# Macaron decoder layer on one core: an attention pipeline with one more step between its first two stages, projection pieces spread over its end, and the convolution's weights loaded behind it

## The chip, the core and the metric

The kernel runs on one core of a Trainium2 chip. The metric is device time in microseconds (us) from the first to the last work of one execution, as the median of three runs. The profile is of a single execution.

## What is computed

One layer of a decoder: SwiGLU feed-forward, a token mixer with two branches, a second feed-forward, each behind an RMSNorm with adaptive shift and scale. The change is in the mixer's attention branch and in the merge of the two branches:

```python
proj = h @ w_in[l]                                   # h: normalised, (1, 1024, 1024)
b_g, c_g, u, q, k, v, z_conv, z_attn = jnp.split(proj, IN_OFFSETS, axis=-1)
y_conv = (b_g * short_conv(c_g * u, conv_w[l])) @ w_conv_proj[l]
q = apply_rope(q.reshape(bsz, s, 16, 64), cos, sin)
k = apply_rope(k.reshape(bsz, s, 4, 64), cos, sin)
y_attn = sliding_window_attention(q, k, v, sinks[l]) @ w_attn_proj[l]
merged = jax.nn.sigmoid(z_conv) * y_conv + jax.nn.sigmoid(z_attn) * y_attn
x = x + gt2[:, None, :] * (merged @ w_out[l])
```

The attention looks back over a window of 128 positions, in blocks of 128 queries; 4 key-value heads serve 16 query heads, and each head has a sink in its softmax.

## The kernel before

All products are float32. Each operand is split into a high and a low part (`split`, L105 to L107: a cast on ACT, then a subtraction on DVE or POOL), and a product is three matmuls (`mm3`, L134 to L142). A weight block of 128 x 1024 comes by `load_w`: SP loads it into a landing buffer with the tag `wr` (four buffers), then two casts and two subtractions write its parts into two other tiles. The landing buffer is free again when the second subtraction is done.

The attention stage runs over 32 units, (g, n): key-value head g and query block n, with n inner. A unit goes through five stages. A (`stage_a`) multiplies the block by the q, k and v weights of the head, DVE applies the rotary factors to the result in PSUM, and POOL adds the two halves (L995) and copies a piece (L996). B (`stage_b`) transposes that on PE (L1010) and splits it. C (`stage_c`) makes the scores (L1031) and the softmax: four rows of DVE (L1042), four of ACT (L1048), then POOL divides (L1060). D (`stage_d`) transposes the probabilities (L1074) and splits them. E (`stage_e`) multiplies by v (L1097, L1098) and splits the result into tiles (L1108, L1109) that four units fill together.

When four units have filled such a tile, eight projection pieces are put into the list `fill`: one piece (`proj_piece`) is 12 matmuls for one of eight output rows db, with weights from a block that serves four pieces; the result is added to `yat` on DVE (L1128). The loop over steps s issues for each step C of unit s-2, B of unit s-1, A of unit s, two pieces, E of unit s-4 and D of unit s-3. Here C(30) stands for C of unit 30, and so on. `conv_proj` (24 matmuls) multiplies the convolution branch by its weights (`load_wc`: four blocks at a time) and merges both branches on DVE with gates that SP loads (L1155 to L1157); `load_y` brings the convolution branch back from DRAM, eight tiles of 512 KB a half.

PE's order is the order of the code. That of DVE, ACT, POOL and SP is worked out when the kernel is built; each engine then takes its rows in that order. Tiles of a tag go to whichever buffer is free.

Of the kernel before, what the change touches and what calls it, by code (L numbers as in the profile page):

```python
# [35 lines left out]
def tile_macaron_layer(  # L36
# [19 lines left out]
    nc = tc.nc  # L56
# [22 lines left out]
    def tile_t(dt=F32R, shape=(P, 2, HALF)):  # L79
        return act.tile(list(shape), dt, tag="T", name=nm("t"), bufs=28)  # L80
# [14 lines left out]
    def f32(t):  # L95
        return t.bitcast(F32)
# [34 lines left out]
    def load_w(src, lo_engine=nc.vector, tiles=None):  # L131
        return Weights(load_st(src), src.shape[1], lo_engine, tiles)
# [821 lines left out]
    with tc.tile_pool(name="att", bufs=2) as tmp:  # L954
# [48 lines left out]
        def stage_b(g, n):  # L1003

            u = st[g, n]
            if n == 0:
                kts[g] = tile_c(F32R), tile_c(F32R)
            o = bank()
            for i in range(3):
                nc.tensor.transpose(  # L1010
                    o[:, i * P : (i + 1) * P], u["r"][:, i * P : (i + 1) * P], ident
                )
            qt = sum_tile(HALF, F32R)
            qh, ql = qt[:, 0:256], qt[:, 256:512]
            split(qh, ql, o[:, 0:256])
            kh, kl = (t[:, n * P : (n + 1) * P] for t in kts[g])
            split(kh, kl, o[:, 256:384])
            u["q"] = (qh, ql)
# [92 lines left out]

        wapt = {}

        def proj_piece(g, h, db):

            if db % 4 == 0:
                wapt[0] = load_w(wap[g, db // 4], nc.gpsimd if db == 0 else nc.vector,
                                 [tile_t(), tile_t()])
            o = bank()
            ah, al = at[g, h]  # L1120
            for pr in range(2):
                c0 = pr * 512 + (db % 4) * P
                mm3([o], wapt[0](c0), [(ah[:, pr, :], al[:, pr, :])],
                    pr == 0, pr == 1)
            if g == 0:
                nc.scalar.copy(yat[db][h], o)
            else:
                nc.vector.tensor_tensor(yat[db][h], yat[db][h], o, op=ALU.add)  # L1128
# [5 lines left out]
        def load_y(h):  # L1134
            for i in range(KT):
                t = tile_t()
                nc.sync.dma_start(f32(t), ycv[i][h])
                yparts[i, h] = pair_of(t)

        def load_wc(dq):  # L1140
            wc[dq] = [load_w(wcp[g, dq]) for g in range(4)]
# [20 lines left out]

        units = [(g, n) for g in range(NKV) for n in range(NB)]
        fill = []
        for s in range(len(units) + 4):
            def at_(k):
                return units[s - k] if 0 <= s - k < len(units) else None
            if at_(2):
                stage_c(*at_(2))
            if at_(1):  # L1170
                stage_b(*at_(1))
            if at_(0):
                g, n = at_(0)
                if n == 0:
                    load_group(g)
                stage_a(g, n)
            if s == len(units):
                load_wc(0)
                load_y(0)
                load_y(1)  # L1180
            for _ in range(2):
                if fill:
                    proj_piece(*fill.pop(0))
            if at_(4):
                stage_e(*at_(4))
                g, n = at_(4)
                if n % 4 == 3:
                    fill += [(g, n // 4, db) for db in range(8)]
            if at_(3):
                stage_d(*at_(3))  # L1190
            if s > len(units):
                conv_proj(s - len(units) - 1, 0)
        for f in fill:
            proj_piece(*f)
        conv_proj(3, 0)
        for db in range(4):
            conv_proj(db, 1)
# [208 lines left out]
```

## Time and profile before

| | |
|---|---|
| median of 3 runs | 2294.13 us (2292.82 to 2300.34) |
| the profiled execution | 2291.84 us, span of its instructions 2289.7 us |
| PE busy | 2206.0 us, 96% of the span |
| DVE, ACT, POOL busy | 1675.7, 1061.9, 395.0 us (73%, 46%, 17%) |
| attention stage, first A to last piece | about 1096 to 1468 us of the span |
| mean granted TensorE clock | 0.988 |

The attention stage is 16% of the span. The shares are means over the whole kernel: where PE waits is read from its list of waits and its timeline.

### The profile page before, as it was taken

The page shows a single profiled execution, that of the slowest core. Times are in us where ns is not written, and L with a number is a line of the kernel's source. Part 1 is how long each engine was busy: PE and PEld are TensorE (multiplying, and loading weights), DVE is VectorE, ACT ScalarE, POOL GpSimd, SP SyncE. Part 2 cuts the span into 40 slices and gives each one's busy share as a digit, 9 for nine tenths or more (in the row PEclk, how much of TensorE's full clock was granted, in tenths as well). Part 3 has the DMA queues.
Part 4 walks back from the last instruction along what each step waited for, and adds up shares of the span by engine and source line. Part 5 has one row for each costly group of instructions (what it writes and reads, how often), then busy time and mean ns, then how long its engine had stood idle before and what let it go on. Part 6 is the DMA issues. An engine that isn't in the chain of part 4 may idle for free.

```text
span 2289.7 us, 30099 instructions
## 1 busy us (share of the span) xinstructions
PE 2206.0 (96%) x10392; PEld 1845.3 (81%) x10392; DVE 1675.7 (73%) x2966; ACT 1061.9 (46%) x2095; POOL 395.0 (17%) x445
## 2 busy tenths in 40 slices
PE   5899999999998999999899997999999999999997
PEld 3688888888887888888889996788888888888786
DVE  8897778767868777777477776554786776676876
ACT  4554444444446443343476555123644444454443
POOL 3000000006452000000344443002100000002644
PEclk9899999999999999999999998999999999999998
DMA  8265456599732543444121115454233553389932
GB/s 322 74 221 172 149 185 212 181 406 299 270 115 106 184 134 107 155 157 155 56 64 57 49 48 212 133 170 155 75 120 120 184 184 120 120 326 343 337 116 74
DMA packets 146744, 381.63 MB, mean 167 GB/s; under 512 B 20384, under 2 KB 22560, under 8 KB 146592
## 3 DMA queue, kind: packets, MB, share of 16 engines
q1 hardware_dynamic: 141984, 371.33, 46.5%
q0 software_dynamic: 4608, 8.39, 2.1%
q8 instruction: 81, 1.33, 0.2%
q14 instruction: 71, 0.58, 0.1%
HBM read 270.61 MB, written 109.05 MB: 166 GB/s over the span
## 4 chain that ended last, share of the span: by engine, by line
PE 86%; DVE 7%; issue 2%; ACT 1%; DMA 1%; POOL 1%; SPq 0%; POOLq 0%; DVEq 0%; ACTq 0%
PE ps L195 60%; PE ps L142 6%; PE ps L140 6%; PE ps L138 6%; PE ps L977 2%; PE ps L975 2%; PE ps L976 2%; DVE w L107 1%; PE ps L1031 1%; PE ps L1074 1%; DVE t L225 1%; DMA wr<-in_w2d_dram 1%; POOL s L319 1%; PE ps L1010 1%; PE ps L1098 1%
## 5 line engine op out<-in xcount | busy, mean ns | idle before, releaser
L195 PE MATMUL ps<-t,w 128*128 128x512 f32 x6468 | 1469.2, 389 | 5.0 <-DVE r L405 3.0
L195 PEld LDWEIGHTS ps<-t,w 128*128 128x128 f32 x6468 | 1213.4, 188 | 260.4 <-DVE r L405 5.8
L106 ACT CAST w<-wr 128x512 fp32r<-128x512 f32 (+1 forms) x420 | 255.3, 613 | 481.2 <-PE ps L195 365.3
L107 DVE TENSOR_TENSOR w<-wr,w 128x512 fp32r<-128x512 f32 (+1 forms) x404 | 304.4, 760 | 137.8 <-ACT w L106 136.2
L515 POOL TENSOR_TENSOR x<-x,g 128x512 f32<-128x512 f32 x96 | 145.2, 1526 | 1061.5 <-DMA t<-hs 941.1
L106 ACT CAST w<-ws 128x512 fp32r<-128x512 f32 x231 | 143.9, 623 | 250.3 <-PE ps L195 200.6
L140 PE MATMUL ps<-t,w 128*128 128x512 f32 (+1 forms) x528 | 204.9, 388 | 6.5 <-DVE t L290 6.5
L107 DVE TENSOR_TENSOR w<-ws,w 128x512 fp32r<-128x512 f32 x231 | 161.4, 703 | 39.4 <-ACT w L106 39.0
L138 PE MATMUL ps<-t,w 128*128 128x512 f32 (+1 forms) x400 | 156.2, 390 | 7.2 <-ACT t L279 7.2
L142 PE MATMUL ps<-t,w 128*128 128x512 f32 (+1 forms) x400 | 154.4, 386 | 1.1 <-DVE w L107 1.1
L140 PEld LDWEIGHTS ps<-t,w 128*128 128x128 f32 x528 | 100.4, 190 | 28.4 <-DVE t L290 9.2
L344 DVE TENSOR_TENSOR x<-x,x 128x512 fp32r<-128x512 f32 x161 | 102.8, 687 | 2.9 <-ACT x L343 2.8
L343 ACT CAST x<-x 128x512 fp32r<-128x512 f32 x161 | 88.8, 624 | 20.4 <-DVE x L431 10.2
L225 DVE CUSTOM_DVE_ANT_0 wr<-wr,crow_act,v 128x1024 f32<-128x1024 f32 x56 | 71.7, 1282 | 36.0 <-DMA wr<-in_wada_dram 35.9
L138 PEld LDWEIGHTS ps<-t,w 128*128 128x128 f32 x400 | 76.4, 191 | 23.9 <-ACT t L279 9.8
L569 DVE SCALAR_TENSOR_TENSOR x<-ps,mods,x 128x512 f32<-128x512 f32 (+1 forms) x104 | 72.9, 706 | 23.6 <-PE ps L195 12.9
L107 POOL TENSOR_TENSOR w<-wr,w 128x512 fp32r<-128x512 f32 (+1 forms) x16 | 21.5, 1358 | 397.3 <-ACT w L106 397.3
L142 PEld LDWEIGHTS ps<-t,w 128*128 128x128 f32 x400 | 76.4, 191 | 16.5 <-DVE w L107 1.8
L319 POOL TENSOR_TENSOR s<-s,q 128x512 f32<-128x512 f32 (+1 forms) x48 | 56.8, 1185 | 188.8 <-ACT q L315 187.3
L975 PE MATMUL ps<-w,t 128*128 128x384 f32 x256 | 88.3, 345 | 0.0
L977 PE MATMUL ps<-w,t 128*128 128x384 f32 x256 | 85.7, 335 | 0.0
L976 PE MATMUL ps<-w,t 128*128 128x384 f32 x256 | 85.6, 335 | 0.0
(150 smaller groups left out, 2815.6 us busy)
## 6 DMA issues: line engine op xcount, KB each, us to landing
t<-hs SPq DMA_DIRECT2D x140, 512.0 KB, 9.9
hs<-x SPq DMA_DIRECT2D x277, 256.0 KB, 4.6
wr<-in_wada_dram SPq DMA_DIRECT2D x56, 512.0 KB, 3.8
wr<-in_w1gu_dram SPq DMA_DIRECT2D x44, 512.0 KB, 4.6
wr<-in_w2gu_dram SPq DMA_DIRECT2D x44, 512.0 KB, 3.6
wr<-in_wbcu_dram SPq DMA_DIRECT2D x24, 512.0 KB, 4.1
wr<-in_w1d_dram SPq DMA_DIRECT2D x22, 512.0 KB, 7.5
wr<-in_w2d_dram SPq DMA_DIRECT2D x22, 512.0 KB, 7.5
```

Source lines behind the costliest of these rows:

```text
L106: nc.scalar.copy(hi, src)
L107: lo_engine.tensor_tensor(lo, src, f32(hi), op=ALU.subtract)
L138: mm(o, wh, xh, start=start, stop=False)
L140: mm(o, wh, xl, start=False, stop=False)
L142: mm(o, wl, xh, start=False, stop=stop)
L195: mm(o, a, b, start=first, stop=last, skip_group_check=True)
L225: nc.vector.tensor_tensor_reduce(out=st, in0=st, in1=crow_act, scale=1.0, scalar=v[:, C_BADA + i : C_BADA + i + 1], op0=ALU.mult, op1=ALU. ...
L344: nc.vector.tensor_tensor(f32r(t), t, f32(hi), op=ALU.subtract)
L515: nc.gpsimd.tensor_tensor(dst, dst, r, op=ALU.add)
L975: mm(o[:, :384], xh, wh, start=k == 0, stop=False)
L976: mm(o[:, :384], xh, wl, start=False, stop=False)
L977: mm(o[:, :384], xl, wh, start=False, stop=k == KT - 1)
```

## The change

Three parts. The loop has one step more between A and B: a step now issues C of unit s-3, B of unit s-2, A of unit s, the pieces, E of unit s-5 and D of unit s-4. The pieces are two a step up to step 28, one a step from step 29 to 32, three a step from 33 to 36. A weight block for pieces is now asked for one block ahead (`next_wap`), right behind the fourth piece of the block before it, and its low part is always made by DVE (before, every second block's was made by POOL). And at the end: `load_y(0)` moves from step 32 to step 29, `load_wc(0)` and `load_y(1)` stand behind the loop, and the first two `conv_proj` stand behind the loop as well, ahead of the last eight pieces, where before the first three were issued in steps 33 to 35.

```diff
--- before.py
+++ after.py
@@ -1111,17 +1111,21 @@
 
         wapt = {}
 
+        def next_wap(g, h, db):
+            wapt["next"] = load_w(wap[g, db // 4], tiles=[tile_t(), tile_t()])
+
         def proj_piece(g, h, db):
 
             if db % 4 == 0:
-                wapt[0] = load_w(wap[g, db // 4], nc.gpsimd if db == 0 else nc.vector,
-                                 [tile_t(), tile_t()])
+                wapt[0] = wapt.pop("next")
             o = bank()
             ah, al = at[g, h]
             for pr in range(2):
                 c0 = pr * 512 + (db % 4) * P
                 mm3([o], wapt[0](c0), [(ah[:, pr, :], al[:, pr, :])],
                     pr == 0, pr == 1)
+            if db % 4 == 3 and fill:
+                next_wap(*fill[0])
             if g == 0:
                 nc.scalar.copy(yat[db][h], o)
             else:
@@ -1162,36 +1166,41 @@
 
         units = [(g, n) for g in range(NKV) for n in range(NB)]
         fill = []
-        for s in range(len(units) + 4):
+        n_units = len(units)
+        for s in range(n_units + 5):
             def at_(k):
-                return units[s - k] if 0 <= s - k < len(units) else None
+                return units[s - k] if 0 <= s - k < n_units else None
+            if at_(3):
+                stage_c(*at_(3))
             if at_(2):
-                stage_c(*at_(2))
-            if at_(1):
-                stage_b(*at_(1))
+                stage_b(*at_(2))
             if at_(0):
                 g, n = at_(0)
                 if n == 0:
                     load_group(g)
                 stage_a(g, n)
-            if s == len(units):
-                load_wc(0)
+            if s == n_units - 3:
                 load_y(0)
-                load_y(1)
-            for _ in range(2):
+
+            for _ in range(2 if s < n_units - 3 else 1 if s <= n_units else 3):
                 if fill:
                     proj_piece(*fill.pop(0))
+            if at_(5):
+                stage_e(*at_(5))
+                g, n = at_(5)
+                if n % 4 == 3:
+                    if not fill:
+                        next_wap(g, n // 4, 0)
+                    fill += [(g, n // 4, db) for db in range(8)]
             if at_(4):
-                stage_e(*at_(4))
-                g, n = at_(4)
-                if n % 4 == 3:
-                    fill += [(g, n // 4, db) for db in range(8)]
-            if at_(3):
-                stage_d(*at_(3))
-            if s > len(units):
-                conv_proj(s - len(units) - 1, 0)
-        for f in fill:
-            proj_piece(*f)
+                stage_d(*at_(4))
+        load_wc(0)
+        load_y(1)
+        conv_proj(0, 0)
+        conv_proj(1, 0)
+        while fill:
+            proj_piece(*fill.pop(0))
+        conv_proj(2, 0)
         conv_proj(3, 0)
         for db in range(4):
             conv_proj(db, 1)
```

How the rows move, on the engines of three places.

PE, start of the attention stage. Names: `ps_9069` is the result of A(0), `q_9098` its rotated q and k. Before, the end of A(0):

```order
L975 MATMUL ps_9069<-w_9064,t_5852 128x384
L976 MATMUL ps_9069<-w_9064,t_5852 128x384
L977 MATMUL ps_9069<-w_9064,t_5852 128x384
L1010 MATMUL ps_9109<-ident,q_9098 128x128 x3
L975 MATMUL ps_9118<-w_9039,t_5810 128x384
```

Now, the end of A(0), the start of A(1), the end of A(1):

```order
L975 MATMUL ps_9069<-w_9064,t_5852 128x384
L976 MATMUL ps_9069<-w_9064,t_5852 128x384
L977 MATMUL ps_9069<-w_9064,t_5852 128x384
L975 MATMUL ps_9107<-w_9039,t_5810 128x384
L976 MATMUL ps_9107<-w_9039,t_5810 128x384
...
L977 MATMUL ps_9107<-w_9064,t_5852 128x384
L1010 MATMUL ps_9147<-ident,q_9098 128x128 x3
L975 MATMUL ps_9156<-w_9039,t_5810 128x384
```

The transposes of B(0) (`q_9098`) stood between A(0) and A(1) and now stand between A(1) and A(2).

SP and ACT, end of the stage. Names: `wr` are landing buffers, `in_wap` blocks of the attention's projection, `in_wcp` of the convolution's projection, `ycv` tiles of the convolution branch (eight rows like the one shown). SP before:

```order
L114 DMA wr_12867<-in_wap_dram 128x1024
L114 DMA wr_13093<-in_wcp_dram 128x1024
...
L114 DMA wr_13101<-in_wcp_dram 128x1024
...
L114 DMA wr_13109<-in_wcp_dram 128x1024
...
L114 DMA wr_13117<-in_wcp_dram 128x1024
L114 DMA wr_13159<-in_wap_dram 128x1024
L114 DMA wr_13335<-in_wap_dram 128x1024
L114 DMA wr_13495<-in_wap_dram 128x1024
L1137 DMA t_13125<-ycv_5926 128x1024
```

SP now:

```order
L114 DMA wr_12995<-in_wap_dram 128x1024
...
L114 DMA wr_13178<-in_wap_dram 128x1024
...
L114 DMA wr_13250<-in_wap_dram 128x1024
...
L114 DMA wr_13339<-in_wap_dram 128x1024
...
L1141 DMA t_12647<-ycv_5926 128x1024
...
L114 DMA wr_13345<-in_wcp_dram 128x1024
L114 DMA wr_13353<-in_wcp_dram 128x1024
L114 DMA wr_13361<-in_wcp_dram 128x1024
L114 DMA wr_13369<-in_wcp_dram 128x1024
L114 DMA wr_13498<-in_wap_dram 128x1024
```

Before, the four convolution blocks went out between the rope tables of the last units, ahead of the last projection blocks; now four projection blocks go out ahead of them, then half 0 of the branch, then the convolution blocks. ACT before, from the split of B(31) (`ws_13088`) to the split of E(28):

```order
L106 CAST ws_13088<-ps_13084 128x256
L1104 COPY s_13027<-ps_13018 64x256
L1048 ACTIVATE t_13064,den_13066<-t_13064,negm_13065 128x256 x4
L106 CAST t_12164<-ps_13084 128x128
L1108 CAST t_12625<-s_13027 128x2x128
L1055 ACTIVATE es_13067<-es_13067 128x4
L106 CAST t_13157<-wr_13159 128x512
L106 CAST t_13158<-wr_13159 128x512
L1104 COPY s_13192<-ps_13183 64x256 x2
L1108 CAST t_13181<-s_13192 128x2x128
```

ACT now, from B(31)'s keys (`t_12202<-ps_13068`) to the cast of the block that the pieces of step 34 use (`t_13176`); `t_13119<-ps_13121` is the split of D(29):

```order
L106 CAST t_12202<-ps_13068 128x128
L1055 ACTIVATE es_13051<-es_13051 128x4
L106 CAST w_13355<-wr_13353 128x512
L106 CAST w_13356<-wr_13353 128x512
L1104 COPY s_13112<-ps_13103 64x256 x2
L1108 CAST t_13101<-s_13112 128x2x128
L106 CAST w_13363<-wr_13361 128x512
L106 CAST w_13364<-wr_13361 128x512
L106 CAST t_13119<-ps_13121 128x512
L106 CAST t_13119<-ps_13128 128x512
L106 CAST t_13176<-wr_13178 128x512
L106 CAST t_13177<-wr_13178 128x512
```

Before, all convolution casts were done ahead of the rows shown; now casts of the second and third convolution block stand ahead of D(29)'s split and of the projection block.

DVE, behind the loop. Names: `x_90..<-..,ps_..` evictions of pieces, `q_` gates and merged rows of conv_proj, `t_13533` and `t_13496` the low part of the last projection block. Before:

```order
L1128 TENSOR_TENSOR x_9025<-x_9025,ps_13433 128x512
L1105 TENSOR_TENSOR s_13450<-s_13450,ps_13441 64x256 x2
L1156 TENSOR_TENSOR x_9020<-x_9020,q_13484 128x512
L1156 TENSOR_TENSOR x_9021<-x_9021,q_13600 128x512
L1155 TENSOR_TENSOR q_13482<-q_13482,ps_13457 128x512
L1157 TENSOR_TENSOR q_13482<-q_13482,x_9020 128x512
L107 TENSOR_TENSOR t_13489<-q_13482,x_13490 128x512
L107 TENSOR_TENSOR t_13533<-wr_13535,t_13533 128x512
L107 TENSOR_TENSOR t_13534<-wr_13535,t_13534 128x512
```

Now (the eviction of the first of the eight last pieces and the first merge of conv_proj 1 stand just ahead):

```order
L1161 TENSOR_TENSOR q_13418<-q_13418,x_9018 128x512
L1160 TENSOR_TENSOR x_9019<-x_9019,q_13456 128x512
L1132 TENSOR_TENSOR x_9027<-x_9027,ps_13473 128x512
L1160 TENSOR_TENSOR x_9020<-x_9020,q_13564 128x512
L1132 TENSOR_TENSOR x_9028<-x_9028,ps_13481 128x512
L1161 TENSOR_TENSOR q_13454<-q_13454,x_9019 128x512
L107 TENSOR_TENSOR t_13425<-q_13418,x_13426 128x512
L1132 TENSOR_TENSOR x_9029<-x_9029,ps_13489 128x512
L1160 TENSOR_TENSOR x_9021<-x_9021,q_13600 128x512
L1160 TENSOR_TENSOR x_9026<-x_9026,q_13636 128x512
L107 TENSOR_TENSOR t_13461<-q_13454,x_13462 128x512
L107 TENSOR_TENSOR t_13496<-wr_13498,t_13496 128x512
```

The last block's low part stood ahead of the evictions of the pieces that follow it; now it stands behind the evictions of the first four of the last eight pieces, mixed with the merges of conv_proj 0 and 1.

## Rows read from the trace of the kernel before

Times are microseconds from the span's start unless marked ns. PE is TensorE, DVE VectorE, ACT ScalarE, POOL GpSimd, SP the engine that issues most DMAs. In a timeline row the first number is the start, the second the duration, "xN" the number of merged instructions, and the bracket the idle time before the row with the operation that ended it. Durations on PE overlap with the next instruction, so distances are read from start to start.

**Rows 1.** Busy time by stretch of the span: stretch, its length, then for PE, PE's weight loads, DVE, ACT and POOL the busy time and (x) the number of instructions, then the granted TensorE clock as a share of full speed, the DMA share and GB/s.
```profile
1100.00:1126.00 26.00, 21.08 (x142) 19.43 (x143) 13.28 (x58) 11.06 (x41) 7.67 (x16) 1.00 0.05 15
...
1160.00:1396.00 236.00, 235.63 (x1544) 215.94 (x1544) 174.51 (x548) 146.72 (x453) 98.58 (x173) 1.00 0.17 49
1396.00:1412.00 16.00, 8.19 (x34) 5.95 (x33) 8.27 (x24) 5.24 (x17) 6.88 (x11) 0.69 1.00 387
1412.00:1433.00 21.00, 17.13 (x88) 13.61 (x87) 11.86 (x28) 8.17 (x22) 3.29 (x6) 0.91 0.62 237
...
1452.00:1468.00 16.00, 14.75 (x50) 11.01 (x51) 11.31 (x15) 2.30 (x5) 2.96 (x2) 0.79 0.53 164
1468.00:1500.00 32.00, 32.00 (x143) 26.50 (x142) 18.00 (x28) 7.42 (x13) 0.00 (x0) 1.00 0.36 111
```

**Rows 2.** What PE waited for between 1080 and 1500: line that waited, releaser, total, times, longest.
```profile
PE ps L138 <- ACT t L106: 11.5, 3, 5.4
PE ps L1010 <- POOL q L995: 4.9, 4, 2.0
PE ps L142 <- POOL t L107: 2.8, 2, 2.4
...
PE ps L1010 <- POOL q L996: 1.1, 1, 1.1
...
PE ps L1098 <- DVE t L107: 0.5, 1, 0.5
```

**Rows 3.** Timeline of PE at the start of the attention stage: the transposes of stage B (L1010) and the first projection piece (L138, L140).
```profile
1101.96 0.63 PE L1010 MATMUL ps<-ident,q 128*128 128x128 f32 x3 [1.98 <-POOL q L995]
...
1122.43 0.63 PE L1010 MATMUL ps<-ident,q 128*128 128x128 f32 x3 [0.70 <-POOL q L995]
...
1138.38 0.33 PE L1010 MATMUL ps<-ident,q 128*128 128x128 f32 x1 [1.13 <-POOL q L996]
...
1159.24 0.50 PE L138 MATMUL ps<-t,t 128*128 128x512 f32 x1 [1.46 <-ACT t L1108]
1160.05 0.50 PE L140 MATMUL ps<-t,t 128*128 128x512 f32 x1 [0.32 <-POOL t L1109]
```

**Rows 4.** Timeline of PE at the end of the attention stage: first matmuls of projection pieces and what follows them.
```profile
1402.97 0.80 PE L138 MATMUL ps<-t,t 128*128 128x512 f32 x1 [5.44 <-ACT t L106]
...
1407.15 0.63 PE L138 MATMUL ps<-t,t 128*128 128x512 f32 x1
1407.58 0.63 PE L140 MATMUL ps<-t,t 128*128 128x512 f32 x1
...
1428.76 0.50 PE L138 MATMUL ps<-t,t 128*128 128x512 f32 x1 [3.28 <-ACT t L106]
...
1452.79 0.51 PE L138 MATMUL ps<-t,t 128*128 128x512 f32 x1 [2.73 <-ACT t L106]
```

**Rows 5.** Timeline of PE in the dense part, the first row of each stage in one step (C is L1031, B L1010, A L975, pieces L138, E L1097, D L1074, and the next step's C), and the first conv_proj behind the last piece.
```profile
1385.91 0.98 PE L1031 MATMUL ps<-t,ws 64*128 64x256 f32 x12
1386.82 0.55 PE L1010 MATMUL ps<-ident,q 128*128 128x128 f32 x3
1387.13 0.42 PE L975 MATMUL ps<-w,t 128*128 128x384 f32 x1
...
1391.38 0.39 PE L138 MATMUL ps<-t,t 128*128 128x512 f32 x1
...
1394.14 0.29 PE L1097 MATMUL ps<-t,vt 128*128 128x256 f32 x1
...
1395.11 1.04 PE L1074 MATMUL ps<-ident,t 128*128 128x128 f32 x8
1396.07 0.98 PE L1031 MATMUL ps<-t,ws 64*128 64x256 f32 x12
...
1467.67 0.39 PE L138 MATMUL ps<-t,w 128*128 128x512 f32 x1
```

**Rows 6.** Timeline of DVE (softmax rows L1042, subtractions L107) and of ACT (casts L106) in the last steps with A, and the cast of the first projection block behind them.
```profile
1387.99 0.48 DVE L1042 CUSTOM_DVE_ANT_0 t<-ps,mask,nsink 128x256 f32<-128x256 f32 x1
...
1388.41 0.48 DVE L1042 CUSTOM_DVE_ANT_0 t<-ps,mask,nsink 128x256 f32<-128x256 f32 x1
...
1396.27 1.28 DVE L107 TENSOR_TENSOR w<-wr,w 128x512 fp32r<-128x512 f32 x2
...
1393.15 1.66 ACT L106 CAST w<-wr 128x512 fp32r<-128x512 f32 x3
...
1402.31 1.13 ACT L106 CAST t<-wr 128x512 fp32r<-128x512 f32 x2
```

**Rows 7.** SP's issue of three projection blocks at the end of the stage; DMA issues from 1300 to 1385 and from 1385 to 1415 (KB each, median us from issue to landing); and the landing of all eight convolution blocks.
```profile
1391.34 4.77 SPq L114 DMA_DIRECT2D wr<-in_wap_dram  x3
...
wr<-in_wap_dram SPq DMA_DIRECT2D x4, 512.0 KB, 4.8
...
t<-ycv SPq DMA_DIRECT2D x16, 512.0 KB, 10.1
wr<-in_wap_dram SPq DMA_DIRECT2D x4, 512.0 KB, 3.7
wr<-in_wcp_dram SPq DMA_DIRECT2D x1, 512.0 KB, 10.9
...
DMA to landing us min/median/max: 3.3/3.6/10.9
```

## The prediction

> **What bounds the kernel now.** I read the share of busy time first and then left it: TensorE (PE) shows work in 96% of the span, so only places where it waits, or runs at its lower clock, can give time back. The table of stretches [rows 1] finds them inside the attention stage: its start, where PE is busy for 21.1 of 26 us; a dense middle, 235.6 of 236; and from 1396 us on 8.2 of 16 at a granted clock of 0.69, with 0.91 and 0.79 in later stretches. From 1468 us on PE is full again. So what this change can win lies between 1100 and 1160 and between 1396 and 1468.
>
> PE's list of waits [rows 2] names the causes. At the start, transposes of stage B wait for Pool: 4.9 + 1.1 = 6.0 us, in five places, the longest and the shortest of the first four and the fifth in [rows 3]. They come because B of a unit stands right behind A of the same unit. At the end, 11.5 us are waits for a cast on ACT, 2.8 for a subtraction on Pool. The casts are of weight blocks for projection pieces: 5.44, 3.28 and 2.73 us, each at a piece's first matmul [rows 4].
>
> One dense step of the middle gives the prices of PE's parts, start to start [rows 5]: C 0.91, B 0.31, A 4.25, two pieces 2.76 (1.38 each), E 0.97, D 0.96. A conv_proj has 24 matmuls of the piece's kind, 24 x 0.23 = 5.52.
>
> The end of the stage now, from 1396.07 to 1467.67 (the first conv_proj behind the pieces), takes 71.6 us. The work in it: 2 C, 1 B, 16 pieces, 4 E, 3 D, 3 conv_proj = 1.8 + 0.3 + 22.1 + 3.9 + 2.9 + 16.6 = 47.6. So 24.0 us are lost there. The listed idle time is 11.5 + 2.8 + 0.5 = 14.8 [rows 2]. The other 9.2 are slow matmuls: behind each of the three long waits they start 0.43 apart for a while, as at 1407.15 [rows 4], instead of 0.23: the lower of the two clock levels. That is 3.1 us for each such wait. Waits up to 1.98 us at the start were not followed by it (granted clock 1.00 there [rows 1]), one of 2.73 was.
>
> **The change, part by part.** *One step deeper.* B of a unit now runs behind A of the next unit, 4.25 us later; the chain that it waits for overran by 0.70 to 1.98 us. So the five waits of B go: -6.1 us. C, D and E keep their distance of one step from each other. Bounds: -4.9 if Pool's copy (the 1.13 one) is late for another reason, -7.8 if the waits of the first piece (1.46 and 0.32, [rows 3]) go as well. I take -6.1, since that piece waits for E, whose distance to it is unchanged.
>
> *Next block prefetched, its subtraction on DVE.* In the middle this costs nothing: PE had no idle time there, and the cast and the subtraction stand behind the softmax rows of DVE as before. DVE gets 2 x 0.65 us more for each of 8 blocks, 10.4 us in all, and in the 236 us it is busy for 174.5 [rows 1]. If that cover failed, 1.3 us would show at each of 8 places.
>
> *Pieces moved.* 16 pieces stay 16 pieces; one instead of two per step from step 29 to 32, three in steps 33 to 36. Steps 32 to 36 have no A. PE's work for them is about 30 us.
>
> *Convolution weights behind the last unit.* This is where I see the new wait. The landing buffers (tag wr) are four. In SP's new order three blocks of the attention projection (wr_13178, 13250, 13339) and wr_12995 are issued before the first convolution block. So all four convolution blocks go one after the other through the one buffer that comes free: each load waits until DVE has subtracted the block before it. And ACT's new order puts casts of these blocks ahead of work that PE needs: behind the cast of the third block stand the split of D(29) and the cast of the next projection block, t_13176. ACT and DVE take their rows in order: the projection block that was loaded at 1391.34 and landed 3.7 later was cast at 1402.31 only, behind a softmax chain [rows 6, 7]. So the chain counts. I add it up from the start of C(29) in step 32 (time 0), with durations of [rows 6]: cast 0.52, subtraction or another row of 512 columns on DVE 0.60 to 0.65, softmax row 0.41; load 3.6 us from issue to landing [rows 7]:
> - DVE reaches the softmax rows 2.1 behind the scores, as in the dense step, needs 1.6 for four, then 1.3 for block t_12993: buffer free at 5.0. Load 1 lands at 8.6, two casts and subtractions end at 10.4.
> - Load 2 lands at 14.0. Casts to 15.1. On DVE a reciprocal and an eviction stand between the two subtractions: 16.6.
> - Load 3 lands at 20.2. Casts to 21.3, split of D(29) to 22.3, first cast of t_13176 at 22.9. DVE goes from 20.8 on through two subtractions, an eviction, half a split, four softmax rows, the other half and the first subtraction of t_13176, 5.5 in sum: 26.3.
> - PE: step 32 is 0.91 + 0.31 + 1.38 + 0.97 + 0.96 = 4.5. C(30) needs the keys' low half, for which DVE has 3.0 of small rows and D(28)'s split to do behind the two new subtractions: 8.0, a wait of 3.2 in all, and C(30) ends at 8.7. Then B, three pieces, E, D, C(31), one piece (8.7 in sum): PE is at t_13176 at 17.4 and, but for two matmuls, goes on at 26.3: a wait of 8.4.
>
> The rest of steps 34 to 36 has no wait by the same count; the fourth block is subtracted at 28, and the first conv_proj comes at 42. *Behind the loop*, the second half of the last projection block is subtracted behind a long row on DVE (evictions of the pieces and of conv_proj 0 and 1, shown above): 14 operations of 0.62 from the end of the first piece, 8.7 us, while PE needs 3 pieces and two matmuls, 4.6: a wait of 4.1 to 4.7, I take 4.4. Of conv_proj's y tiles and gates nothing is late: PE does not read the gates, and half 1 of y is read some 25 us after its loads.
>
> New waits 3.2 + 8.4 + 4.4 = 16.0. Lower clock behind the last two, 2 x 3.1 = 6.2; behind the first it only uses up time in which PE would wait anyway. The end loses 22.2 instead of 24.0: -1.8. Bounds: each load 3.3 to 4.8 us [rows 7] moves the middle wait by -0.9 to +3.6; no lower clock takes 6.2 off.
>
> **Sum.** -6.1 - 1.8 = -7.9. The profiled execution took 2291.84 (span 2289.7): 2283.9. The median of the runs shown is 2294.13, 2.3 above it: 2286.2. A change of under 0.3% (6.9 us) can't be told from none here.
>
> [...] The Trainium skill, "TensorE: Matmul & The Clock Gate", in "Architectural detail", says that the queues of ScalarE and VectorE are strict first in, first out; by that rule a cast whose load hasn't landed holds everything behind it, and it speaks against this order. The trace agrees: the cast at 1402.31 came some 7 us after its load had landed. [...]
>
> **Rivals.** *The prefetch pays in full:* blocks that are loaded early hide their latency, the chain through one buffer ends before PE is there, and the 8.4 us wait with its slow matmuls does not come: 2286.2 - 11.5 = 2274.7. For it: in the dense middle this buffering hides every load [rows 1]. Against it: four loads through one buffer can't overlap. The Trainium skill, "Trainium Kernel Development and Optimization", "Best Practices", has this as its rule: double-buffer, so that DMA and compute overlap.
>
> *No difference:* the loads take 4.8 like the projection blocks of [rows 7], +3.6, which gives 2290; or the early waits stay because Pool is late for another reason, +6.1, which gives 2292. For it: the fifth wait was for Pool's copy (L996), not for the sum ahead of it [rows 2], so Pool's own queue has a part. Against it: 4.25 us of cover where 1.98 was the longest wait.
>
> *Slower:* the four convolution blocks land like the one that was queued with the y tiles, in 10.9 instead of 3.6 [rows 7]: three loads, +21.9, 2308. It decides from 8.5 us a load ((7.9 + 6.9) / 3 above 3.6). For it: load_y(0) now stands ahead of them in SP's order. Against it: its buffers come free four steps earlier, and 8 tiles take about 10 us.
>
> **How the numbers follow.** Forecast 0.50, with 2282 to 2291 as its own range; prefetch in full 0.18; no difference 0.22; slower 0.10. Faster by over 0.3% is below 2287.2: 0.30 of the forecast's half, the 0.18, and 0.02 of the third: 0.50. Within 0.3%: 0.40. Slower: 0.10. The range reaches from 2274 (the second case) to 2294 (the top of the third) and leaves out the slower case and some of the ends.
>
> **What would show it.** No wait of B for Pool at the start of the stage; PE's next-longest list led by a wait of a piece for a cast on ACT of about 6 us and, right behind it, for DVE; convolution loads one at a time, 6 us apart; the clock down behind it and behind the last block. Wrong, if the convolution blocks are cast without a wait for their loads, if A of the next unit does not cover Pool, or if waits appear in the dense middle.

## The result, and the profile after

The changed kernel takes 2281.14 us (median of five runs, 2279.57 to 2283.49) against 2294.13: a ratio of 0.9943 (95% interval 0.9930 to 0.9956), 13 us faster. The forecast was 2286.2, with a range of 2274 to 2294. Profile against profile, the span goes from 2289.7 to 2277.8.

The stretches of the attention stage after the change, which answer to [rows 1] (stretch, length, busy us and instructions of PE, PE's weight loads, DVE, ACT, POOL, then the granted clock, DMA share, GB/s):
```profile
1100.00:1126.00 26.00, 26.00 (x176) 24.92 (x175) 14.14 (x62) 11.31 (x42) 9.22 (x19) 1.00 0.08 22
...
1160.00:1378.00 218.00, 217.68 (x1444) 200.61 (x1443) 168.19 (x523) 136.77 (x424) 86.98 (x155) 1.00 0.20 64
1378.00:1394.00 16.00, 13.15 (x98) 11.11 (x98) 13.79 (x41) 12.65 (x39) 4.46 (x7) 1.00 0.22 67
1394.00:1420.00 26.00, 17.94 (x86) 13.80 (x83) 19.57 (x43) 13.53 (x33) 6.08 (x10) 0.80 0.38 126
1420.00:1452.00 32.00, 28.22 (x115) 22.57 (x115) 18.58 (x30) 3.91 (x9) 2.00 (x2) 0.89 0.79 288
1452.00:1490.00 38.00, 38.00 (x169) 31.49 (x168) 20.68 (x32) 7.98 (x14) 0.00 (x0) 1.00 0.38 119
```
The start is full now (26.0 of 26 us, before 21.1), the middle stayed full, and the end still has a hole with a low clock. PE's waits between 1080 and 1500 (line that waited, releaser, total, times, longest), which answer to [rows 2]:
```profile
PE ps L138 <- ACT t L106: 7.6, 2, 5.5
PE ps L142 <- DVE t L107: 4.1, 3, 2.2
PE ps L1031 <- ACT t L106: 2.1, 1, 2.1
PE ps L975 <- DVE vt L1000: 1.2, 1, 1.2
...
PE ps L1031 <- DVE t L107: 0.8, 1, 0.8
```
The waits of B (L1010) for Pool are gone, and so are the waits of pieces for Pool. Casts on ACT lead, with subtractions on DVE behind them. Where they stand on PE, in the order of time, beside the marks by which I measure the stage (the first A, E of unit 23, C(29), the first conv_proj behind the last piece):
```profile
1096.08 0.33 PE L975 MATMUL ps<-w,t 128*128 128x384 f32 x1
...
1144.76 0.44 PE L975 MATMUL ps<-w,t 128*128 128x384 f32 x1 [1.17 <-DVE vt L1000]
...
1351.01 0.29 PE L1097 MATMUL ps<-t,vt 128*128 128x256 f32 x1
...
1378.33 0.39 PE L1031 MATMUL ps<-t,ws 64*128 64x256 f32 x2
...
1385.06 0.38 PE L1031 MATMUL ps<-t,ws 64*128 64x256 f32 x2 [2.07 <-ACT t L106]
1386.23 0.85 PE L1031 MATMUL ps<-t,ws 64*128 64x256 f32 x10 [0.78 <-DVE t L107]
...
1401.54 0.79 PE L138 MATMUL ps<-t,t 128*128 128x512 f32 x1 [5.52 <-ACT t L106]
...
1404.99 0.79 PE L142 MATMUL ps<-t,t 128*128 128x512 f32 x1 [2.23 <-DVE t L107]
1405.58 0.63 PE L138 MATMUL ps<-t,t 128*128 128x512 f32 x1
1406.01 0.63 PE L140 MATMUL ps<-t,t 128*128 128x512 f32 x1
...
1441.42 0.50 PE L138 MATMUL ps<-t,t 128*128 128x512 f32 x1 [2.07 <-ACT t L106]
...
1443.86 0.79 PE L142 MATMUL ps<-t,t 128*128 128x512 f32 x1 [1.71 <-DVE t L107]
...
1451.74 0.39 PE L138 MATMUL ps<-t,w 128*128 128x512 f32 x1
```
The same marks before:
```profile
1095.63 0.33 PE L975 MATMUL ps<-w,t 128*128 128x384 f32 x1
...
1354.42 0.29 PE L1097 MATMUL ps<-t,vt 128*128 128x256 f32 x1
```
The end mark of before is the 1467.67 of [rows 5]. From these comes the account. Before: 372.04 us from first A to end mark. After: 355.66, and 5.52 on top, since one conv_proj fewer lies ahead of the mark: 361.18, or **-10.9 in the stage**. Split at E of unit 23: before it 258.79, after it 254.93, less the 4.25 of one A more that the deeper pipeline has put ahead of it: **-8.1 in the start and middle**, and so **-2.7 in the tail**. The other 1 us of the span lies outside the stage, where nothing was changed. In the profiles of the kernels below the stretch behind the stage differs by 5 us (818.9 to 824.4) and the one ahead of it by as much (first A at 1093.9 to 1099.3), the start and middle by less than 0.1 where its code is the same. So I read the experiments by the stage, and the medians beside it. One thing limits that: the lower clock can come or stay away behind the same wait, which is worth up to 1.6 us (last section).

### The profile page after: what moved, and what is told of

Its sections match the earlier page's. It is cut to its first block, busy times and chain, and to the rows that moved or that the text cites. A ratio compares the mean times of both kernels' runs of the same rounds, so it can differ in the third digit from the quotient of the medians.

```text
span 2277.8 us, 30045 instructions
## 1 busy us (share of the span) xinstructions
PE 2202.4 (97%) x10392; PEld 1844.5 (81%) x10392; DVE 1682.2 (74%) x2982; ACT 1062.8 (47%) x2095; POOL 382.5 (17%) x429
## 4 chain that ended last, share of the span: by engine, by line
PE 88%; DVE 8%; DMA 2%; issue 1%; ACT 1%; POOL 1%; SPq 0%; POOLq 0%; DVEq 0%; ACTq 0%
PE ps L195 61%; PE ps L142 6%; PE ps L138 6%; PE ps L140 6%; PE ps L977 2%; PE ps L976 2%; PE ps L975 2%; DVE w L107 1%; PE ps L1031 1%; PE ps L1074 1%; DVE t L225 1%; DMA wr<-in_w2d_dram 1%; DVE t L107 1%; PE ps L1010 1%; POOL s L319 1%
## 5 line engine op out<-in xcount | busy, mean ns | idle before, releaser
L106 ACT CAST w<-wr 128x512 fp32r<-128x512 f32 (+1 forms) x420 | 254.9, 612 | 484.7 <-PE ps L195 364.5
L107 DVE TENSOR_TENSOR w<-wr,w 128x512 fp32r<-128x512 f32 (+1 forms) x404 | 303.8, 759 | 141.7 <-ACT w L106 140.4
L106 ACT CAST w<-ws 128x512 fp32r<-128x512 f32 x231 | 143.5, 621 | 249.1 <-PE ps L195 200.3
L140 PE MATMUL ps<-t,w 128*128 128x512 f32 (+1 forms) x528 | 205.7, 390 | 5.6 <-DVE t L290 5.6
L107 DVE TENSOR_TENSOR w<-ws,w 128x512 fp32r<-128x512 f32 x231 | 160.4, 698 | 40.1 <-ACT w L106 39.7
L138 PE MATMUL ps<-t,w 128*128 128x512 f32 (+1 forms) x400 | 156.9, 392 | 7.0 <-ACT t L279 7.0
L140 PEld LDWEIGHTS ps<-t,w 128*128 128x128 f32 x528 | 100.9, 191 | 27.9 <-DVE t L290 8.3
L138 PEld LDWEIGHTS ps<-t,w 128*128 128x128 f32 x400 | 76.7, 192 | 24.1 <-ACT t L279 9.6
L975 PE MATMUL ps<-w,t 128*128 128x384 f32 x256 | 88.2, 345 | 1.2 <-DVE vt L1000 1.2
L107 POOL TENSOR_TENSOR w<-wr,w 128x512 fp32r<-128x512 f32 (+1 forms) x16 | 21.5, 1355 | 398.6 <-ACT w L106 398.6
```

Of the source, the lines that this page charges most:

```text
L106: nc.scalar.copy(hi, src)
L107: lo_engine.tensor_tensor(lo, src, f32(hi), op=ALU.subtract)
L138: mm(o, wh, xh, start=start, stop=False)
L140: mm(o, wh, xl, start=False, stop=False)
L975: mm(o[:, :384], xh, wh, start=k == 0, stop=False)
```

## The experiments

All kernels, with the median, the ratio to the kernel before (run beside each on the same chip) and its 95% interval, and the stage against before, by the marks above. The kernel before had a median of 2293.39 to 2294.82 beside them, so kernels are best compared by the ratio. The tail of e8_filler holds 5.5 us of added work:

| kernel | median us | ratio | start and middle | tail |
|---|---|---|---|---|
| changed | 2281.14 | 0.9943 (0.9930 to 0.9956) | -8.1 | -2.7 |
| e1_deeper | 2284.96 | 0.9962 (0.9948 to 0.9975) | -8.4 | -0.1 |
| e2_flat | 2290.17 | 0.9985 (0.9976 to 0.9994) | +5.4 | -8.7 |
| e11_prefetch | 2283.29 | 0.9957 (0.9943 to 0.9972) | +5.4 | -15.1 |
| e12_wcin | 2278.22 | 0.9931 (0.9918 to 0.9943) | -8.1 | -6.8 |
| e3_tland | 2278.41 | 0.9937 (0.9924 to 0.9949) | -8.1 | -5.8 |
| e4_last | 2274.51 | 0.9922 (0.9910 to 0.9935) | -8.1 | -10.2 |
| e5_both | 2275.71 | 0.9914 (0.9901 to 0.9927) | -8.1 | -11.9 |
| e6_cover | 2277.53 | 0.9926 (0.9914 to 0.9938) | -8.1 | -9.3 |
| e7_all | 2272.95 | 0.9907 (0.9894 to 0.9920) | -8.1 | -11.3 |
| e8_filler | 2279.77 | 0.9939 (0.9926 to 0.9951) | -8.1 | -4.9 |
| e9_early | 2271.61 | 0.9901 (0.9887 to 0.9916) | -4.3 | -19.9 |
| e10_wc34 | 2271.35 | 0.9902 (0.9886 to 0.9919) | -4.4 | -18.7 |

**Which part wins what.** My theory was that the deeper step wins the start and the rest is about even; the rival, that the tail's new order wins.

> The kernel before with the deeper pipeline alone: B, C, D and E one step later, and the conv weights' loads and the conv_projs of the loop one step later with them; no prefetch, two pieces per step. Theory (the start's five waits of B for Pool are what the deeper step wins, the tail is about even): B's waits are gone and the time falls by 6 to 8 us against before, to 2286 to 2288; the tail still loses its 24 us to waits for casts and to slow matmuls. Rival (the gain lies in the tail's new order, the start's waits only move to another place): within 2 us of before, 2292 to 2294.

> The changed kernel with the pipeline's distances as before (B one step behind A, and the steps' counts of pieces shifted with it); prefetch, counts of pieces and conv weights behind the last unit stay. Theory: the start's five waits of B are back (6 us of them), the tail loses some 21 us as in the changed kernel: 2 to 4 us faster than before, 2290 to 2292. Rival (the gain lies in the tail's order): 11 to 13 us faster than before, 2281 to 2283.

```diff
 (e1_deeper, against before)
+            if at_(3):
+                stage_c(*at_(3))
             if at_(2):
-                stage_c(*at_(2))
-            if at_(1):
-                stage_b(*at_(1))
+                stage_b(*at_(2))
...
 (e2_flat, against the changed kernel)
-            if at_(3):
-                stage_c(*at_(3))
             if at_(2):
-                stage_b(*at_(2))
+                stage_c(*at_(2))
+            if at_(1):
+                stage_b(*at_(1))
...
-            for _ in range(2 if s < n_units - 3 else 1 if s <= n_units else 3):
+            for _ in range(2 if s < n_units - 4 else 1 if s < n_units else 3):
```
The medians came out close to the theory, 8.4 (6 to 8 expected) and 3.2 us under the kernel before. But the stage shows that the second number is a sum of two large ones. Without the deeper step, the other parts cost 5.4 us ahead of the mark (there the prefetch alone is at work), and win 8.7 behind it. The price falls due where the weights of the next head are loaded, at three places (1.4, 0.9 and 3.0 us). The first in e2_flat is C of that step; the block's cast on ACT, its subtraction on DVE, then C on PE:
```profile
1148.82 1.14 ACT L106 CAST t<-wr 128x512 fp32r<-128x512 f32 x2
...
1151.35 1.29 DVE L107 TENSOR_TENSOR t<-wr,t 128x512 fp32r<-128x512 f32 x2
...
1155.19 0.38 PE L1031 MATMUL ps<-t,ws 64*128 64x256 f32 x2 [0.50 <-ACT t L106]
1156.97 0.93 PE L1031 MATMUL ps<-t,ws 64*128 64x256 f32 x10 [1.40 <-DVE t L107]
```
C waits for the keys' split, which now comes behind the early block's rows as well as those of the head's weights on ACT and DVE. With B a whole A earlier, nothing of that is seen: e1_deeper and the changed kernel are equal up to the mark (-8.4 and -8.1).

**The prefetch by itself, and the conv weights' place.**

> The kernel before with the prefetch alone: next block loaded and split behind the last piece of the block ahead, its low part on DVE; distances, counts of pieces and conv weights as before. Theory (nothing in the dense middle, where PE has no idle time; in the tail the casts of the later blocks still stand behind the splits of the conv_projs on ACT): 0 to 3 us faster than before, 2290 to 2294. Rival (the early loads are what makes the tail shorter): 6 us or more, under 2288.

```diff
 (e11_prefetch, against before)
-                wapt[0] = load_w(wap[g, db // 4], nc.gpsimd if db == 0 else nc.vector, ...)
+                wapt[0] = wapt.pop("next")
...
+            if db % 4 == 3 and fill:
+                next_wap(*fill[0])
```
The rival was right: the prefetch alone is faster by 0.43%, 10 us. PE's waits in the tail of e11_prefetch (1400 to 1465):
```profile
PE ps L138 <- ACT t L1108: 4.7, 1, 4.7
PE ps L1031 <- DVE t L107: 0.9, 1, 0.9
PE ps L1098 <- DVE t L107: 0.6, 1, 0.6
```
No piece waits for its weights any more: the three long waits of [rows 4] and those for subtractions on Pool are gone, and one for E's cast has come. The tail wins 15.1 of the 24.0 us that it lost. The changed kernel has the same prefetch, and its tail wins 2.7. Ahead of the mark e11_prefetch loses 5.4 as e2_flat does, but the equal sums are chance: the three places cost 1.4, 1.0 and 1.5 here, and the other 1.6 is lower clock at A(1) (granted clock 0.72 from 1105 to 1111), before any block is loaded early.

> The changed kernel with the convolution weights loaded in the loop, in the first step without A, as before, instead of behind the last unit; all else as changed. Theory (the four loads then land in four buffers at once and the chain is gone, but their eight casts stand between the exponentials of a unit on ACT): no wait of 5 us at t_13176, other waits of some 3 us in steps 31 to 33; 2 to 8 us off the changed kernel, 2273 to 2279. Rival (keeping them behind the last unit is what makes the tail no longer than before): 2 us or more above it, 2283 and up.

```diff
+            if s == n_units:
+                load_wc(0)
...
-        load_wc(0)
         load_y(1)
```
4.0 us came back in the tail (by the medians 2.9, which the intervals alone would not settle): the convolution weights behind the last unit cost, they don't win. The wait of 5 us at t_13176 was gone, as the theory had it, with others of 1.0 to 1.9 at a piece, E and C in steps 32 and 33.

**What makes the tail's waits.**

> The changed kernel, with the four blocks of convolution weights landing in four tiles of tag T instead of in the buffers of tag wr; nothing is left out. Theory (the serial chain of four loads through one landing buffer, with the casts in order on ACT, makes the waits of C(30) and of the piece on t_13176): both waits go, 2.9 + 7.8 us, and the slow matmuls behind the second, some 3 us: 13 us off the changed kernel, 2268; less if the first conv_proj now waits for its blocks (they land late, up to 3 us). Rival (the piece waits because ACT and DVE have too much to do in those steps, not for the chain): the two waits stay within 2 us of what they were, 2279 to 2282.

```diff
-            wc[dq] = [load_w(wcp[g, dq]) for g in range(4)]
+            land = [tile_t() for _ in range(4)]
+            raw = [f32(t).rearrange("p a b -> p (a b)") for t in land]
+            for g in range(4):
+                nc.sync.dma_start(raw[g], wcp[g, dq])
+            wc[dq] = [Weights(r) for r in raw]
```
Half of it held. At the first piece on t_13176 the wait for the cast fell from 5.52 to 0.32:
```profile
1395.70 0.50 PE L138 MATMUL ps<-t,t 128*128 128x512 f32 x1 [0.32 <-ACT t L106]
...
1398.83 0.80 PE L142 MATMUL ps<-t,t 128*128 128x512 f32 x1 [2.40 <-DVE t L107]
```
So the chain of loads made that wait. It did not make the other two: the wait for the subtraction stayed (2.40), and C(30) still waited 2.9 us, which I had put on the chain in the expectation although the prediction had counted it from DVE's own rows. Of the 5.9 us won in step 34 half was lost again: 1.6 to slow matmuls behind C(30), 1.1 at conv_proj 0, whose weights now land late, 0.2 at the last pieces. Those still took 18 us.

> The changed kernel, with the second half of the last projection block loaded and split ahead of the first two conv_projs instead of behind the first piece; nothing is left out. Theory (that block is late because its cast stands behind the splits of two conv_projs on ACT and its subtraction in a long row on DVE): the two waits of 3.8 us at the last pieces go and with them some 3 us of slow matmuls: 6 to 7 us off the changed kernel, 2274 to 2275. Rival (the slow matmuls there do not come from this wait): 3.8 us, 2277; or none, if another operand of these pieces is late next.

```diff
+        first = wapt.pop("next")
+        next_wap(*fill[4])
+        wapt["next"], wapt["after"] = first, wapt["next"]
         load_y(1)
         conv_proj(0, 0)
```
As expected: 2274.51. In the changed kernel ACT takes the last block behind the splits of both conv_projs, which wait for their gates, 7 us after the pieces have begun at 1433.75. DVE's first merge of conv_proj 0, then the rows on ACT:
```profile
1431.87 0.69 DVE L1159 TENSOR_TENSOR q<-q,ps 128x512 f32<-128x512 f32 x1 [7.12 <-DMA q<-gate]
...
1440.23 0.62 ACT L106 CAST x<-q 128x512 fp32r<-128x512 f32 x1 [2.38 <-DVE q L1161]
1440.76 1.14 ACT L106 CAST t<-wr 128x512 fp32r<-128x512 f32 x2
```
The eight last pieces and their waits took 17.99 us in the changed kernel and take 10.88 here, with no wait and no slow matmul: 3.8 of wait and 3.3 of lower clock. The first row adds something to the prediction, which let the gates go because PE does not read them: DVE does. It sat idle until the gate landed at 1431.87, some 3.5 us after PE had finished conv_proj 0, and so the merges fell among the last pieces. What an earlier gate alone would give was not run.

> The changed kernel with both edits of e3_tland (convolution blocks landing in T tiles) and e4_last (last projection block ahead of the conv_projs). Theory (e3_tland won 5.9 us at the piece on t_13176 and gave most of it back at the last block, whose cast stood behind the splits of conv_proj 0, which wait for their gates; with that block cast ahead, the give-back can't happen): 4 us less than e4_last, 2270 to 2271. Rival (the give-back is the gates' and convolution blocks' late transfers, which hold conv_proj itself): as e4_last, 2274 to 2276.

The two edits together. By the stage this is 1.7 us better than e4_last (-20.0 against -18.3), not 4: step 34 gains 4.0, and conv_proj 0 and 1 lose 2.3, with 1.6 of waits for their own weights. The expectation named the wrong place for what e3_tland gave back; its rival named the right one. The medians (2275.71 and 2274.51) can't tell the two apart; by them the rival holds.

> The changed kernel with the 16 late pieces dealt out otherwise: none in steps 29 to 31, where A of a unit still fills the time, and 3, 4, 4, 3, 2 in steps 32 to 36. Theory (C(30), t_13176 and its subtraction are late because steps 32 and 33 give PE only 4.5 and 7.5 us of work, less than the chain of a unit on DVE, ACT and Pool, some 8 us): C(30)'s 2.9 us go, the 7.8 us at t_13176 shrink to 0 to 3, with the slow matmuls: 8 to 12 us off the changed kernel, 2269 to 2273. Rival (the convolution blocks' chain of loads sets the tail, whatever PE does meanwhile): the wait moves to a later row and the time stays within 2 us, 2279 to 2283.

> e5_both and e6_cover together: convolution blocks landing in T tiles, last projection block ahead of the conv_projs, pieces dealt out 0, 0, 0, 3, 4, 4, 3, 2. Theory (the tail's loss of 21 us is these three causes and nothing else): all of PE's waits between 1378 and 1452 us go but some 2 us, and the lower clock with them: 18 to 21 us off the changed kernel, 2260 to 2263. Rival (when these waits go, another operand is late next, such as the conv blocks that now land later against PE): 2264 to 2270.

```diff
-            for _ in range(2 if s < n_units - 3 else 1 if s <= n_units else 3):
+            late = [0, 0, 0, 3, 4, 4, 3, 2]
+            for _ in range(2 if s < n_units - 3 else late[s - n_units + 3]):
```
More work in the steps without A did take C(30)'s wait away, and shrank the one at t_13176 from 7.8 to 3.8, but the stage won 6.6 and the median 3.6 us, less than expected, because each block is now needed sooner: waits of 1.1 and 2.8 at the blocks ahead of and behind it. On top of e5_both it won nothing in the stage (e7_all: -19.4 for -20.0; the medians, 2272.95 and 2275.71, point the other way, with intervals that overlap), and e7_all stayed above both of its expectations. Through e3_tland, e5_both, e6_cover and e7_all one number stays: 2.40 for the subtraction of t_13176.

> e7_all with each projection block loaded and split as soon as the first piece of the block ahead of it starts, instead of behind that block's last piece. Theory (the subtraction of t_13176, 2.4 us late in every variant, is late because it is written behind the softmax rows of C(31) on DVE; written earlier it stands ahead of them): the 1.2 + 2.4 + 1.4 us of waits for DVE and the slow matmuls behind them go, 5 to 7 us off e7_all, 2266 to 2268. Rival (DVE has too little time in these steps whatever the order): the wait moves to C or E and the time stays at 2271 to 2274.

> e9_early with the convolution blocks' loads written in step 34 instead of behind the last step. Theory (conv_proj 0 waits 2.4 us for them because they are issued behind two other loads that wait for a landing buffer): 2 to 4 us less than e9_early. Rival (their casts then stand ahead of the splits of D(30) and D(31) on ACT, and E waits): 0 to 4 us more than e9_early.

```diff
 (e9_early, against e7_all)
             if db % 4 == 0:
                 wapt[0] = wapt.pop("next")
...
+                else:
+                    ahead()      # next_wap of the next block in fill
...
-            if db % 4 == 3 and fill and "next" not in wapt:
-                next_wap(*fill[0])
...
 (e10_wc34, against e9_early)
+            if s == n_units + 2:
+                load_wc(0)
...
-        load_wc(0)
```
In e9_early all waits of pieces for weights go; what PE still waits for in the tail (1370 to 1445) are two operands of conv_proj 0:
```profile
PE ps L142 <- DVE w L107: 2.0, 1, 2.0
PE ps L138 <- ACT w L106: 0.4, 1, 0.4
```
The tail has then given back 19.9 of 24.0. So the order on DVE, not its load, made the 2.40. But the same early split in the middle costs 3.8 us there (first pieces wait for E's cast on ACT again, and E and D come late in some steps), so 4.8 us are left against e7_all in the stage and 1.3 by the medians (2271.61), with intervals that overlap; the expected 2266 to 2268 was missed. e10_wc34 is the rival's case: conv_proj no longer waits, E and D do (1.6 and 0.8, granted clock 0.86 there), and the sum is the same by the medians and 1.1 worse in the stage. e9_early and e10_wc34 have the lowest times that were run, 23 us below before and 10 below the changed kernel; from e7_all the intervals don't part them. Early splits in the tail alone were not run.

**The lower clock.**

> The changed kernel with 24 more matmuls of a piece's kind, 5.5 us, on operands that are there, in the place where PE waits for t_13176; their result is not used. Theory (the slow matmuls behind that wait come from PE having been idle, and cost 3 us): the wait for the cast goes to nothing, the one for the subtraction stays at some 2, and since PE has been busy the matmuls behind it start 0.23 apart: 2 to 4 us off the changed kernel, 2277 to 2279, although there is more work. Rival (the lower clock does not come from this wait, or costs nothing): as the changed kernel, 2280 to 2282.

```diff
+            if fill_at == (g, h, db):
+                o = bank()
+                for i in range(8):
+                    mm3([o], wapt[0](0), [(ah[:, 0, :], al[:, 0, :])], i == 0, i == 7)
```
In the changed kernel the three pieces of step 34 take 14.80 us (18 matmuls: a piece is six, and the 12 given with the kernel before are two pieces): 4.14 of work, 7.75 of waits, 2.9 of slow matmuls. Here they take 11.20 with 24 matmuls more: 9.66 of work, 1.24 of wait, 0.3 of slow matmuls:
```profile
1404.06 0.50 PE L142 MATMUL ps<-t,t 128*128 128x512 f32 x1 [1.24 <-DVE t L107]
1404.62 0.40 PE L140 MATMUL ps<-t,t 128*128 128x512 f32 x1
```
So the slow matmuls there do come from PE having waited, and cost 2.9. The stage won 2.1, not 3.6: the pieces behind C(30)'s wait ran slow in this run and had not in the changed kernel's. The median, 2279.77 with runs from 2275 to 2284, is too wide to decide.

## Why the prediction held, and where its steps did not

The sign, the range and the mechanism of the tail held. Three readings did not: that the first piece's wait stays, that the prefetch costs nothing in the middle, and that short waits bring no lower clock (last section). The stage gave 10.9 us for the 7.9 of the sum; the other 2 of the 13 lie outside the edited code and between single runs.

**The chain of loads** came out to within 0.5 us. SP's issues of the first three convolution loads, ACT's casts behind them, and DVE's first subtraction of t_13176:
```profile
1383.35 0.33 SPq L114 DMA_DIRECT2D wr<-in_wcp_dram  x1
...
1389.27 0.33 SPq L114 DMA_DIRECT2D wr<-in_wcp_dram  x1
...
1395.41 0.33 SPq L114 DMA_DIRECT2D wr<-in_wcp_dram  x1
```
```profile
1387.03 1.14 ACT L106 CAST w<-wr 128x512 fp32r<-128x512 f32 x2 [1.53 <-DMA wr<-in_wcp_dram]
...
1392.74 1.14 ACT L106 CAST w<-wr 128x512 fp32r<-128x512 f32 x2 [0.28 <-DMA wr<-in_wcp_dram]
...
1398.86 1.14 ACT L106 CAST w<-wr 128x512 fp32r<-128x512 f32 x2 [1.26 <-DMA wr<-in_wcp_dram]
...
1400.86 1.15 ACT L106 CAST t<-wr 128x512 fp32r<-128x512 f32 x2
...
1404.25 1.28 DVE L107 TENSOR_TENSOR t<-wr,t 128x512 fp32r<-128x512 f32 x2
```
Counted from C(29) at 1378.33, the loads start at 5.0, 10.9 and 17.1 (predicted 5.0, 10.4, 16.6), t_13176 is cast from 22.5 (22.3) and subtracted by 26.6 (26.3). Each cast of a convolution block waited for its load, and t_13176, whose own load had been issued long before, stood behind the third: the in-order rule of the Trainium skill ("TensorE: Matmul & The Clock Gate", "Architectural detail"), which the prediction weighed against this change, in this trace at 5.5 us. The waits: 2.85 at C(30) (3.2 predicted), 7.75 at t_13176 (8.4), 3.78 at the last block (4.4), 14.4 in sum for 16.0; the lower clock 2.9 and 3.3 behind the last two for 6.2. The tail is -2.7 for -1.8.

**The start was undersized**: -8.1 for -6.1. B's waits went as predicted. The step that failed is "that piece waits for E, whose distance to it is unchanged": the first piece's waits of [rows 3] went too, and even the upper bound of 7.8 was passed. Counted from the first A to the rows of D behind each place, the five places of B give 7.2 us, more than the 6.1 of idle time listed for them, and the first piece gives 2.1. The distance in steps is unchanged, but what stands ahead of E's cast on ACT is not. ACT before, up to the cast of E(3), the last row:
```profile
1151.73 1.33 ACT L106 CAST w<-wr 128x384 fp32r<-128x384 f32 x3
...
1154.87 1.16 ACT L106 CAST t<-wr 128x512 fp32r<-128x512 f32 x2
...
1158.78 0.41 ACT L1108 CAST t<-s 128x256 fp32r<-128x256 f32 x1
```
Between the casts of E(2) (at 1147.11) and of E(3) stand eight casts of the next head's weights (the first row is the last three) and two of the piece's own, and on DVE eight subtractions of the same weights. In the changed kernel they come one unit earlier, behind E(1)'s cast (the first row), and that of E(3) (the last) comes in time:
```profile
1136.85 0.41 ACT L1108 CAST t<-s 128x256 fp32r<-128x256 f32 x1 [0.16 <-DVE s L1105]
1137.16 0.51 ACT L106 CAST w<-wr 128x384 fp32r<-128x384 f32 x1
...
1141.47 1.33 ACT L106 CAST w<-wr 128x384 fp32r<-128x384 f32 x3
...
1155.65 0.41 ACT L1108 CAST t<-s 128x256 fp32r<-128x256 f32 x1
```
It ends at 1156.1, the piece comes at 1156.4. The burst of the head's weights, with its subtractions on DVE, now delays vt there instead: the one new wait of 1.17 at A (1144.76), which takes 1.4 of the gain back.

**The prefetch was not nothing.** "In the middle this costs nothing" holds only under the deeper step's cover; alone it costs 3.9 (e11_prefetch, without the 1.6 at A(1)) to 5.4 (e2_flat, lower clock included). Its worth in the tail I did not state by itself at all, only the waits that replace the old ones. Alone it is worth 15.1 there (e11_prefetch). In the stage, the deeper step and the prefetch by themselves give -8.5 and -9.6, and both with the other two parts -10.9. The deeper step takes away the prefetch's price ahead of the mark (-8.1 there with both) and does nothing in the tail (-0.1 alone), so what is lost lies in the tail: -15.1 with the prefetch alone, -2.7 with everything. The 12.4 us between are what the tail's new order costs, if the parts add there. Two of its causes were measured, each by itself: 4.0 for the convolution weights' place (e12_wcin), and 7.1 for the last block behind two conv_projs (e4_last), which e11_prefetch, with a conv_proj in each of the last steps, does not have. Together 11.1; the remaining 1.3 is open, and the deeper step and the prefetch without the rest were not run, so the split is argued, not shown.

**The rivals.** The case in which the prefetch pays in full, 2274.7, did not come, for the reason given against it, but it was sized by one wait only; breaking the chain alone does not bring it (e3_tland), the last block has to be early as well (e4_last, e5_both). No difference: the fifth wait, for Pool's copy (L996), went with the other four. Slower: the seven convolution loads between 1370 and 1440 took 3.6 us in the median, not 10.9:
```profile
wr<-in_wcp_dram SPq DMA_DIRECT2D x7, 512.0 KB, 3.6
```

## What to carry to other kernels

When a change has several parts, forecast and try each part alone as well as the sum: here a sum within its range hid one part worth 15 us in the tail and another that gave most of it back. Where loads share a landing buffer and an engine takes its rows in order, write down that engine's rows around the place: the wait is made by what stands ahead of the row, and moving one block's split ahead of two conv_projs (e4_last) was worth 7 us. When a wait goes, look for the next operand that is just as late before counting the whole of it as won.

## What the runs showed that I had not expected

The lower clock does not follow every wait of the same length. Behind C(30)'s wait of 2.07 and 0.8 the next matmuls ran at 0.23 apart in the changed kernel (4.21 us for 18) and at 0.43 for a while in e3_tland, e4_last and e5_both (5.56, 5.78 and 5.54 for the same 18; the granted clock was 0.73 to 0.75 there, and 1.00 in the changed kernel). In e4_last that took nothing from the sum, as the prediction argued for this place: the wait at t_13176 behind it was 6.22 for 7.75. In e3_tland, where that wait was gone, it cost 1.6. In e11_prefetch the A behind B's wait of 1.98 took 5.94 us; in the kernel before, behind the same wait, 4.36. So "up to 1.98 us no lower clock", as the prediction read it from one trace, is not a rule, and 1 to 2 us of difference between two profiles can be this alone.
